# ScalarE in program order through the token-major projections and the indexer of a hybrid decoder step

## The chip, the cores and the metric

The kernel runs on 1 core of one Trainium2 chip. The metric is the device time of one execution in microseconds (us), as the median of several executions. Its instructions sit on five engines with a queue each: TensorE (PE in the profile, with its weight loads as PEld), VectorE (DVE), ScalarE (ACT), GpSimd (POOL) and SyncE (SP). Which engine an instruction belongs to is fixed by the source. The order in which an engine takes its instructions is fixed when the program is built.

## The reference, cut to what matters

One inference step of a 2-layer decoder trunk runs over 1104 tokens of width 1024: 16 meta tokens, 1024 prompt tokens, and 8 sequences of 8 new tokens. Each layer projects the normalised input, runs three mixers, and merges them:

```python
(aq, af, ai, az, b_glu, bz, cq, ck, cv, cqi, cki, cw, cz, gate) = project(h, norm_g, w_in, b_in)
a, g = jnp.split(glu_in, 2, axis=-1)          # conformer_conv, on b_glu
u = a * jax.nn.sigmoid(g)
y = lax.conv_general_dilated(xp, conv_w[:, None, :], ...)      # 31 taps, depthwise, 512 channels
...
qi = rope(cqi.reshape(nb, nt, IDX_HEADS, IDX_DIM), pos)        # 4 heads of 64
ki = rope(cki[:, :, None, :], pos)[:, :, 0]                    # one key head of 64
...
s = jnp.einsum('bqhd,bsd->bqhs', qi, ki)                       # index_scores
scores = jnp.einsum('bqhs,bqh->bqs', jax.nn.relu(s), wi * IDX_SCALE)
idx, valid = select_keys(scores, allowed, n_sel)               # top 256 of the allowed keys
```

The scores pick, for each token, the 256 keys that the sparse attention then reads.

## The kernel before

TensorE works in fp32 through split operands. An operand X is stored as a rounded part and the rest (XH and XL for activations, wh and wl for weights), and a product is three matmuls: wh on XH, wh on XL, wl on XH. ScalarE makes the rounded part by a copy (L269 for the weights of the big projection, L671 for those of the token-major one, L743 for the indexer's keys), GpSimd or ScalarE the rest (L270, L672, L734, L744).

**The stream.** `stream` is a generator that walks over the chunks of the input projection, 128 output channels each. A chunk has three groups of tokens (384, 384 and 336 columns, `g` 0 to 2), a group 24 matmuls (L391), and every third matmul ends in a `yield`. Those three matmuls are called a step here; a group has 8 steps. Behind the 24th matmul ScalarE evicts the group from PSUM into the tile `sp` with bias and activation (L204, called from L394), and behind group 2 ScalarE itself issues the DMA that writes the chunk to DRAM (`fD`). PSUM has two buffers for the groups (`mm`), so a group can't start before the eviction of the group two back has ended.

**Fill.** Everything else of a layer runs in between. `fill(key)` pulls a number of steps from the stream, given by the table `FILL`, so that TensorE has work while another engine prepares what it needs next.

**Taps.** The convolution is VectorE work: 31 taps for each of 4 channel chunks, a tap being two instructions (L1495 on the prompt, L1496 on the samples). `taps(key)` is called between other VectorE work and pulls taps up to a budget in the table `SIDE` ("tr" after each rope of the token-major projections, "tk" and "ti" in the indexer, "ts" in its sample part). At the start of a chunk `gated` loads the two halves of the GLU (`up` and `cy`), ScalarE takes the sigmoid of `cy` in place (`act_(y, y, AF.Sigmoid)`), and GpSimd multiplies. The tile `cy` has two buffers.

**Token-major projections.** `cproj` computes q, k and weights of the indexer and keys and values with tokens on partitions: 2 groups of 290 columns (`gi`) by 9 tiles of tokens (`t`), each 24 matmuls (L679 to L681) into a PSUM buffer from a small ring, a copy by ScalarE into `CTr` (L684), and the bias by GpSimd (L685). For `gi` 1 VectorE then applies the rope (L718 to L722) and pulls taps.

**Indexer.** `indexer` first splits the keys (tile `kk`, named rl in the trace: L733 on ScalarE, L734 on GpSimd), transposes them (L739), and copies them to KIH and KIL (L743, L744, 12 copies). Then come six blocks of 128 queries (`i` from 7 to 2), each with 4 heads. A head is matmuls into the tile `lg` (L770, L771), the next block's transposes when `h == 1` (`qstack`, L757 to L765), `fill("is")` with 6, 4, 7, 6, 7 or 7 steps, and only then the Relu on ScalarE into `rl` (L204), taps, and the weighted sum into `SC` on VectorE (L803 for head 0, L805 for the others). `lg` has one PSUM buffer at this place, so the matmuls of a head wait for the Relu of the head before. `rl` has two buffers. In the source the order is:

```python
fill("is", 7 - i)
rl = xt.tile([128, 1152], F32, name="rl", tag="rl")
act_(rl[:, 0:n], ps[:, 0:n], AF.Relu)
taps("ti", 7 - i)
```

**What sets the order.** TensorE keeps the order in which the source calls its instructions. VectorE does so from the first tap on (`manual_schedule`). For ScalarE, GpSimd and SyncE a scheduler in the compiler chooses the order by its own estimates. Semaphores keep the data right in any order.

Of the kernel before, what the change touches and what calls it, by code (L numbers as in the profile page):

```python
# [11 lines left out]
def _quiet(msg, *args, **kwargs):  # L12
# [10 lines left out]
AF = mybir.ActivationFunctionType  # L23
# [26 lines left out]
SIDE = {"t0": (5000, 10000, 10000, 10000, 9300, 10000), "tr": (4200, 4200, 4200, 4200, 4200, 4200, 4200, 2000, 0),  # L50
# [3 lines left out]
KSEL = 4  # L54
# [100 lines left out]
def trunk(tc, a, o, depth=DEPTH):  # L155
# [47 lines left out]
    def act_(out, in_, fn, **kw):  # L203
        S.activation(out, in_, fn, **kw)  # L204
# [72 lines left out]
    def wpair(l, blk):  # L277
        wh, wl = weights(l, blk)
        return [(lambda k, j=j: wh[:, 2 * k + j, :], lambda k, j=j: wl[:, 2 * k + j, :]) for j in range(2)]
# [61 lines left out]
    def stream(l, pv, chunks, groups, slot, early, lead, more):  # L341


        n = len(chunks)
        blocks = chunks + [("early", (c, bi)) for c in range(8) for bi in range(2)]
        parts = [(c, g) for g in range(3) for c in range(lead)]
        parts += [(i, g) for i in range(lead, n - 2) for g in range(3)]
        parts += [(i, g) for g in range(3) for i in (n - 2, n - 1)]
        parts += [(i, g) for i in range(n, n + 16) for g in range(3)]
        ws, bufs = {}, {}  # L350

        def get(i):
            if i < len(blocks) and i not in ws:
                nm, c = blocks[i]
                if nm == "early":
                    ws[i] = ws[i - 2][1:] if c[0] % 2 else wpair(l, BLK["pb" if c[1] else "pa"] + c[0] // 2)
                else:
                    ws[i] = wchunk(l, BLK[nm] + c, V if i == lead else G, more if 1 < i < lead else None)

        get(0)  # L360
        get(1)
        yield True
        for i, g in parts:
            if g == 0 and 0 < i < lead - 1:
                get(i + 1)
            if lead <= i < n - 1 or i >= n or (i in (lead - 1, n - 1) and g == 2):
                get(i + 1)
            nm, c = blocks[i]
            if nm == "early":
                yield from early.part(c[1], c[0], g, ws[i][0], slot[0])  # L370
                continue
            bcol = BCOL[nm]
            wh, wl = ws[i]
            if g == 0:
                bufs[i] = spt(more if 1 < i < lead else None)
            n0, nn = groups(nm)[g]
            ps = slot[0]()[:, 0:nn]
            sl = slice(n0, n0 + nn)
            H, L = ([x[:, k, sl] for k in range(8)] for x in (XH, XL))
            if i == 0:  # L380

                ops = []
                for k in range(10):
                    if k < 8:
                        ops += [(wh(k), H[k]), (wl(k), H[k])]
                    if k > 1:
                        ops.append((wh(k - 2), L[k - 2]))
            else:
                ops = [(wh(k), x[k]) for k in range(8) for x in (H, L)] + [(wl(k), H[k]) for k in range(8)]
            for j, (w, x) in enumerate(ops):  # L390
                T.matmul(ps, w, x, start=(j == 0), stop=(j == 23))  # L391
                if j == 23:

                    fn = AF.Sigmoid if nm == "gate" and c < 16 else AF.Identity  # L394
                    act_(bufs[i][:, sl], ps, fn, bias=pv[:, bcol + c:bcol + c + 1])
                    if nm in ("cz",):

                        if g == 0:
                            sg = spt()
                        act_(sg[:, sl], ps, AF.Sigmoid, bias=pv[:, bcol + c:bcol + c + 1])  # L400
                        G.tensor_tensor(bufs[i][:, sl], bufs[i][:, sl], sg[:, sl], op=OP.mult)
                    if g == 2:
                        lo = groups(nm)[0][0]
                        S.dma_start(fD[nm][c, :, lo:NT], bufs[i][:, lo:NT])
                    if i == n - 1:
                        early.load(g)
                if j % 3 == 2:
                    yield True

    class Side:  # L410
# [4 lines left out]
        def __call__(self, key, j=0):  # L415
            ns = SIDE[key] if isinstance(key, str) else key
            self.debt += ns[j] if isinstance(ns, tuple) else ns
# [155 lines left out]
    def layer(l, hst, late):  # L573
# [35 lines left out]
        taps = Side(conv(l, pv, cw, cvp))  # L609
# [3 lines left out]
        slot[0] = mmt  # L613
        ctp = ctr.enter_context(tc.tile_pool(name="ctr", bufs=1, side="right"))
        CTr = ctp.tile([128, 9, 580], F32, name="CTr", tag="CTr")
        cproj(l, CTr, taps)
        scp = scs.enter_context(tc.tile_pool(name="scp", bufs=1))
        SC = scp.tile([128, SCN], F32, name="SC", tag="SC")
        SC8 = scp.tile([128, NT], F32, name="SC8", tag="SC8")
        fill("ic")  # L620
        indexer(l, CTr, SC, SC8, fill, taps)
        ctr.close()
        tk1 = tks.enter_context(tc.tile_pool(name="tk1", bufs=1))
        steps, F = topk(SC, SC8, tk1)
# [30 lines left out]
        return merge(l, pv, late_groups, fill, ers)  # L655


    def cproj(l, CTr, taps):
        with tc.tile_pool(name="cpk", bufs=CPK, side="right") as cpk, tc.tile_pool(name="cpr", bufs=2, side="right") as cpr, \
                tc.tile_pool(name="cpt", bufs=2, side="right") as cpt:  # L660
            for gi, (c0, w) in enumerate(CGROUPS):
                brep = cpr.tile([128, 290], F32, name="brep", tag="brep")
                Y.dma_start(brep[:, 0:w], a["b_in"][l, c0:c0 + w].partition_broadcast(128))
                ch, cl = [], []
                for k2 in range(4):
                    cr = cpr.tile([128, 2, 290], F32, name="cr", tag="cr")
                    Y.dma_start(cr[:, :, 0:w], a["wc"][l, gi, k2])
                    for k in range(2):
                        h_ = cpk.tile([128, 290], F32R, name="ch", tag="ch")
                        l_ = cpk.tile([128, 290], F32R, name="cl", tag="cl")  # L670
                        S.copy(h_[:, 0:w], cr[:, k, 0:w])  # L671
                        G.tensor_tensor(l_[:, 0:w], cr[:, k, 0:w], f(h_[:, 0:w]), op=OP.subtract)  # L672
                        ch.append(h_)
                        cl.append(l_)
                for t in range(9):
                    rows, ts = TROWS[t], slice(128 * t, 128 * t + TROWS[t])
                    ps = dmt()
# [786 lines left out]
    def conv(l, pv, cw, c1):  # L1464
        def gated(c):
            up = c1.tile([128, 1070], F32, name="up", tag="up", bufs=2)
            us = c1.tile([128, 8, 38], F32, name="us", tag="us", bufs=2)
            y = c1.tile([128, NT], F32, name="cy", tag="cy", bufs=2)
# [4 lines left out]
            Y.dma_start(y, fD["gg"][c])  # L1473
            Y.dma_start(sr[:, 0], a["state_conv"][l, c])
            G.tensor_copy(us[:, :, 0:30], sr[:, 0])
            act_(y, y, AF.Sigmoid)
            G.tensor_tensor(up[:, 30:1070], up[:, 30:1070], y[:, 0:1040], op=OP.mult)
            G.tensor_tensor(us[:, :, 30:38], us[:, :, 30:38], y[:, 1040:1104].rearrange("p (b q) -> p b q", q=8), op=OP.mult)

# [6 lines left out]
        for c in range(4):  # L1486
            up, us, y = nxt
            yp, ys = y[:, 0:1040], y[:, 1040:1104].rearrange("p (b q) -> p b q", q=8)
            for j in range(31):
                w = cw[:, j, c:c + 1]  # L1490
# [285 lines left out]
```

## Time and profile before

| | |
|---|---|
| time, median of 3 runs | 2926.06 us (2922.28 to 2927.58) |
| the profiled execution's own time | 2926.8 us |
| its span in the profile | 2924.9 us |
| TensorE clock granted, mean | 0.979 of full speed |
| busy share of the span | PE 94%, PEld 90%, DVE 72%, ACT 41%, POOL 43% |

The profile is of one execution. Its own time exceeds its span by 1.9 us of start and end. A busy PE is one with a matmul in its pipeline; the table says that PE seldom stands without one, not how fast it goes. The times below count from the span's start. Layer 0's token-major projections begin at 127.8 us, layer 1's at 1572.5 us.

### The profile page before, as it was taken

How to read it: one execution, taken by the hardware profiler on the slowest of the kernel's cores; microseconds unless marked ns; L12 is line 12 of the kernel's file. 1: busy time of each engine (PE TensorE's matmuls, PEld its weight loads, DVE VectorE, ACT ScalarE, POOL GpSimd, SP SyncE). 2: the span in 40 equal slices, each digit the busy share in tenths (PEclk: the TensorE clock that was granted, in tenths of full speed). 3: DMA queues.
4: the chain of work that ended last, by engine and by line, in shares of the span. 5: the costliest groups of instructions: out<-in, count | busy, mean ns of one | idle time of the engine just before them, and what ended most of it. 6: DMA issues, size and time to landing. Idle time of an engine off the chain costs nothing. (4 is left out here: it accounts for less than half of the span.)

```text
span 2924.9 us, 44993 instructions
## 1 busy us (share of the span) xinstructions
PE 2757.9 (94%) x17094; PEld 2620.9 (90%) x17094; DVE 2113.7 (72%) x3832; ACT 1186.8 (41%) x2369; POOL 1247.6 (43%) x978
## 2 busy tenths in 40 slices
PE   7989899999998999999999998998999999999898
PEld 7988879999998888879999997898999989988798
DVE  5798867889969667535366896788899786774443
ACT  4314443323333556544341334422332335565432
POOL 3533334434425214756564332443434241157563
PEclk9999999999999999999999999999999999999999
DMA  4523234332335124666453322323332441247554
GB/s 146 162 61 109 90 103 140 122 112 89 118 130 170 67 67 154 195 201 197 150 169 105 98 83 90 127 99 109 130 112 77 157 151 63 86 150 222 190 166 148
DMA packets 192569, 374.14 MB, mean 128 GB/s; under 512 B 30657, under 2 KB 129697, under 8 KB 192289
## 3 DMA queue, kind: packets, MB, share of 16 engines
q1 hardware_dynamic: 166016, 272.21, 29.7%
q10 hardware_dynamic: 20448, 78.09, 6.6%
q0 software_dynamic: 5888, 20.97, 2.3%
q8 instruction: 134, 2.20, 0.3%
q14 instruction: 83, 0.67, 0.1%
HBM read 251.07 MB, written 122.40 MB: 128 GB/s over the span
## 5 line engine op out<-in xcount | busy, mean ns | idle before, releaser
L391 PE MATMUL mm<-xh,wh 128*128 128x384 f32 (+2 forms) x2656 | 888.1, 336 | 27.6 <-ACT sp L204 23.9
L391 PE MATMUL mm<-xl,wh 128*128 128x384 f32 (+2 forms) x2656 | 886.0, 336 | 0.0
L270 POOL TENSOR_TENSOR wl<-wr,wh 128x512 fp32r<-128x512 f32 x332 | 473.1, 1443 | 697.8 <-ACT wh L269 465.8
L391 PEld LDWEIGHTS mm<-xh,wh 128*128 128x128 f32 x2656 | 506.0, 191 | 41.5 <-ACT sp L204 29.0
L391 PE MATMUL mm<-xh,wl 128*128 128x384 f32 (+2 forms) x2656 | 531.3, 336 | 0.0
L391 PEld LDWEIGHTS mm<-xl,wh 128*128 128x128 f32 x2656 | 506.2, 191 | 7.2 <-issue 1.9
L391 PEld LDWEIGHTS mm<-xh,wl 128*128 128x128 f32 x2656 | 461.8, 192 | 6.3 <-issue 1.9
L916 DVE TENSOR_SCALAR_CACHE_REDUCE jk<-SC,F 80x1104 bf16<-80x1104 f32 (+6 forms) x448 | 448.8, 1002 | 8.4
L204 ACT ACTIVATE sp<-mm,vec 128x384 f32<-128x384 f32 (+1 forms) x356 | 198.6, 564 | 512.0 <-PE mm L391 494.8
L1495 DVE SCALAR_TENSOR_TENSOR cy<-up,vec,cy 128x1040 f32<-128x1040 f32 x240 | 337.9, 1408 | 0.4
L269 ACT CAST wh<-wr 128x512 fp32r<-128x512 f32 x352 | 203.6, 618 | 164.1 <-PE mm L391 80.4
L204 ACT ACTIVATE P<-P,nm 128x896 f32<-128x896 f32 (+7 forms) x128 | 99.5, 778 | 64.1 <-DVE nm L1021 61.7
L1037 DVE TENSOR_TENSOR pl<-tp,ph 128x512 fp32r<-128x512 f32 x144 | 97.8, 687 | 36.9 <-ACT ph L1036 36.1
L1496 DVE SCALAR_TENSOR_TENSOR cy<-us,vec,cy 128x64 f32<-128x64 f32 x240 | 117.2, 488 | 0.0
L1036 ACT CAST ph<-tp 128x512 fp32r<-128x512 f32 x144 | 83.2, 584 | 54.4 <-PE tp L1033 50.2
L1021 DVE CUSTOM_DVE_ANT_0 P<-sc,MB 128x512 f32<-128x512 f32 (+1 forms) x96 | 63.9, 667 | 57.1 <-PE sc L1015 56.2
L1346 PEld LDWEIGHTS lg<-hQ,hK 128*128 128x128 f32 x512 | 65.8, 205 | 28.0 <-issue 19.9
L1025 DVE TENSOR_SCALAR P<-P,nm 128x896 f32<-128x896 f32 (+7 forms) x128 | 87.4, 683 | 4.3
L1346 PE MATMUL lg<-hQ,hK 128*128 128x64 f32 x512 | 66.4, 286 | 25.5 <-DVE hQ L1375 25.3
L1033 PE MATMUL tp<-ident,P 128*128 128x128 f32 x576 | 88.0, 275 | 1.5 <-DVE P L1025 1.5
L204 ACT ACTIVATE rl<-lg 128x1024 f32<-128x1024 f32 (+6 forms) x54 | 42.6, 788 | 102.8 <-DVE SC L805 60.2
L287 PE MATMUL tp<-xh,wh 128*128 128x384 f32 (+2 forms) x240 | 79.9, 335 | 0.4 <-DVE z L1681 0.4
(454 smaller groups left out, 5932.0 us busy)
## 6 DMA issues: line engine op xcount, KB each, us to landing
wr<-in_wp SPq DMA_DIRECT2D x180, 512.0 KB
eg<-gateD SPq DMA_DIRECT2D x80, 184.0 KB
gateD<-sp ACTq DMA_DIRECT2D x24, 552.0 KB
gateD<-sp ACTq DMA_DIRECT2D x24, 544.0 KB
cr<-in_wc SPq DMA_DIRECT2D x16, 290.0 KB
gt<-gateD SPq DMA_DIRECT2D x24, 192.0 KB
za<-zaD SPq DMA_DIRECT2D x24, 192.0 KB
ggD<-sp ACTq DMA_DIRECT2D x8, 552.0 KB
```

Source lines behind the costliest of these rows:

```text
L204: S.activation(out, in_, fn, **kw)
L269: S.copy(wh[:, k:k + 4], wr[:, k:k + 4])
L270: (eng or G).tensor_tensor(wl[:, k:k + 4], wr[:, k:k + 4], f(wh[:, k:k + 4]), op=OP.subtract)
L391: T.matmul(ps, w, x, start=(j == 0), stop=(j == 23))
L916: V.tensor_scalar(jk[0:rows, 0:n], s, F.bitcast(F32)[0:rows, j:j + 1], None, op0=OP.is_ge, op1=OP.add, accum_out=cnt[0:rows, j:j + 1])
L1025: V.tensor_scalar(p[:, 0:n], p[:, 0:n], nm[:, 3:4], None, op0=OP.mult)
L1033: T.transpose(ps[:, 128 * c:128 * c + 128], P[c][:, 128 * kt:128 * kt + 128], ident)
L1036: S.copy(ph, ps)
L1037: V.tensor_tensor(pl, ps, f(ph), op=OP.subtract)
L1346: T.matmul(ps[:, 64 * c:64 * c + 64], K[:, 128 * c:128 * c + 128], up(Q[:, 128 * c:128 * c + 128], m), start=True, stop=True)
L1495: V.scalar_tensor_tensor(yp, up[:, j:j + 1040], w, yp, op0=OP.mult, op1=OP.add)
L1496: V.scalar_tensor_tensor(ys, us[:, :, j:j + 8], w, ys, op0=OP.mult, op1=OP.add)
```

## The change

Five things are edited. ScalarE's instructions are put under `manual_schedule`, hence in the order of the source, from the first eviction of the token-major projections to the end of the indexer. `cproj` is cut in two loops: the first, outside that order, loads and splits the weights of both groups, the second does the matmuls. For the convolution's chunks 2 and 3 the sigmoid of the GLU's gate half moves from `gated` to the eviction of the projection (`nm == "gg" and c >= 2`), so that DRAM holds the sigmoid already. `SIDE["tr"]` falls by 1000 for each rope, and `SIDE["ts"]` rises by 1000, which moves taps from between the ropes to the indexer's sample part. The lines behind L671 shift by 3 to 8 (in the indexer by 7: L733 is L740 after).

```diff
--- before.py
+++ after.py
@@ -47,8 +47,8 @@
         "hl": (5, 6, 5, 5, 9, 6, 16), "hk": 2, "hs": (0, 1, 0, 1, 0, 1, 0, 4), "ho": 2, "ht": 10, "c0": 59,
         "c1": (13, 22, 52), "aq": 16, "av": (2, 2, 2, 2, 2, 1, 3, 2), "a0": 6, "as": (3, 1, 1, 1, 2, 1, 0, 1),
         "mp": (3, 3, 3), "tl": 3, "tk": 4, "ts": (1, 2, 0, 2, 2), "tt": (0, 0, 1, 4, 6), "tp": (2, 2, 2, 1, 4, 3), "to": 1}
-SIDE = {"t0": (5000, 10000, 10000, 10000, 9300, 10000), "tr": (4200, 4200, 4200, 4200, 4200, 4200, 4200, 2000, 0),
-        "tk": 4200, "ti": (1400, 2800, 2800, 2800, 2800, 2800), "ts": 3000,
+SIDE = {"t0": (5000, 10000, 10000, 10000, 9300, 10000), "tr": (3200, 3200, 3200, 3200, 3200, 3200, 3200, 1000, 0),
+        "tk": 4200, "ti": (1400, 2800, 2800, 2800, 2800, 2800), "ts": 4000,
         "na": (5000, 5000, 5000, 2000, 0, 0, 0, 2000, 1300), "hd": 3000, "hl": (5500, 1000, 2500, 2500, 3700, 4200, 8000),
         "hs": 1000, "hk": 5000, "ho": 500, "ht": 2000, "he": 6500, "c0": 3500, "cc": 1200, "c1": 6000}
 KSEL = 4
@@ -391,7 +391,7 @@
                 T.matmul(ps, w, x, start=(j == 0), stop=(j == 23))
                 if j == 23:
 
-                    fn = AF.Sigmoid if nm == "gate" and c < 16 else AF.Identity
+                    fn = AF.Sigmoid if (nm == "gate" and c < 16) or (nm == "gg" and c >= 2) else AF.Identity
                     act_(bufs[i][:, sl], ps, fn, bias=pv[:, bcol + c:bcol + c + 1])
                     if nm in ("cz",):
 
@@ -613,12 +613,14 @@
         slot[0] = mmt
         ctp = ctr.enter_context(tc.tile_pool(name="ctr", bufs=1, side="right"))
         CTr = ctp.tile([128, 9, 580], F32, name="CTr", tag="CTr")
-        cproj(l, CTr, taps)
+        act = ExitStack()
+        cproj(l, CTr, taps, act)
         scp = scs.enter_context(tc.tile_pool(name="scp", bufs=1))
         SC = scp.tile([128, SCN], F32, name="SC", tag="SC")
         SC8 = scp.tile([128, NT], F32, name="SC8", tag="SC8")
         fill("ic")
         indexer(l, CTr, SC, SC8, fill, taps)
+        act.close()
         ctr.close()
         tk1 = tks.enter_context(tc.tile_pool(name="tk1", bufs=1))
         steps, F = topk(SC, SC8, tk1)
@@ -655,9 +657,10 @@
         return merge(l, pv, late_groups, fill, ers)
 
 
-    def cproj(l, CTr, taps):
+    def cproj(l, CTr, taps, act):
         with tc.tile_pool(name="cpk", bufs=CPK, side="right") as cpk, tc.tile_pool(name="cpr", bufs=2, side="right") as cpr, \
                 tc.tile_pool(name="cpt", bufs=2, side="right") as cpt:
+            groups = []
             for gi, (c0, w) in enumerate(CGROUPS):
                 brep = cpr.tile([128, 290], F32, name="brep", tag="brep")
                 Y.dma_start(brep[:, 0:w], a["b_in"][l, c0:c0 + w].partition_broadcast(128))
@@ -672,6 +675,10 @@
                         G.tensor_tensor(l_[:, 0:w], cr[:, k, 0:w], f(h_[:, 0:w]), op=OP.subtract)
                         ch.append(h_)
                         cl.append(l_)
+                groups.append((gi, c0, w, brep, ch, cl))
+
+            act.enter_context(tc.manual_schedule(engines={mybir.EngineType.Activation}))
+            for gi, c0, w, brep, ch, cl in groups:
                 for t in range(9):
                     rows, ts = TROWS[t], slice(128 * t, 128 * t + TROWS[t])
                     ps = dmt()
@@ -1473,7 +1480,8 @@
             Y.dma_start(y, fD["gg"][c])
             Y.dma_start(sr[:, 0], a["state_conv"][l, c])
             G.tensor_copy(us[:, :, 0:30], sr[:, 0])
-            act_(y, y, AF.Sigmoid)
+            if c < 2:
+                act_(y, y, AF.Sigmoid)
             G.tensor_tensor(up[:, 30:1070], up[:, 30:1070], y[:, 0:1040], op=OP.mult)
             G.tensor_tensor(us[:, :, 30:38], us[:, :, 30:38], y[:, 1040:1104].rearrange("p (b q) -> p b q", q=8), op=OP.mult)
```

TensorE's order is the same in both kernels. VectorE's differs in where taps stand; between the first rope and the last there are 22 before and 16 after. Outside the stretches named above the orders of ScalarE and GpSimd are the same.

ScalarE in layer 0, from the last weight split before the token-major projections to the key split `kk` (`rl<-CTr`). The kernel before:

```order
L684 COPY CTr<-tp 128x290 x2
L204 ACTIVATE cy<-cy 128x1104
L684 COPY CTr<-tp 128x290
L684 COPY CTr<-mm 128x290 x2
L684 COPY CTr<-tp 80x290
L684 COPY CTr<-tp 128x290 x2
L684 COPY CTr<-mm 128x290 x2
L684 COPY CTr<-tp 128x290 x3
L684 COPY CTr<-mm 128x290
L684 COPY CTr<-mm 80x290
L204 ACTIVATE sp<-mm,vec 128x384 x2
L733 CAST rl<-CTr 128x8x64
```

The changed kernel, from the third copy of `gi` 1 on:

```order
L691 COPY CTr<-mm 128x290 x2
L691 COPY CTr<-tp 128x290 x3
L691 COPY CTr<-mm 128x290
L691 COPY CTr<-mm 80x290
L269 CAST wh<-wr 128x512 x2
L204 ACTIVATE sp<-mm,vec 128x384 x2
L204 ACTIVATE sp<-mm,vec 128x336
L404 DMA vD<-sp 128x1104
L269 CAST wh<-wr 128x512 x2
L204 ACTIVATE sp<-mm,vec 128x384
L740 CAST rl<-CTr 128x8x64
L740 CAST rl<-CTr 80x64
```

The sigmoid `cy<-cy`, which stood before between the copies L684, is gone. All three evictions of the first chunk behind the projections, the next chunk's weight split and the first eviction of that chunk now stand ahead of `kk`, where before only two evictions did.

ScalarE in the heads of block `i` 7 (`rl` of 1024 columns; `qs` are the transposed queries). The kernel before:

```order
L404 DMA afD<-sp 128x1104
L204 ACTIVATE rl<-lg 128x1024
L204 ACTIVATE sp<-mm,vec 128x384
L204 ACTIVATE rl<-lg 128x1024
L762 CAST qs<-tp 64x2x128
L763 CAST qs<-tp 64x2x128
L204 ACTIVATE cy<-cy 128x1104
L204 ACTIVATE sp<-mm,vec 128x384
L204 ACTIVATE rl<-lg 128x1024
L269 CAST wh<-wr 128x512 x2
L204 ACTIVATE rl<-lg 128x1024
L204 ACTIVATE sp<-mm,vec 128x336
```

The changed kernel:

```order
L269 CAST wh<-wr 128x512 x2
L204 ACTIVATE sp<-mm,vec 128x384
L204 ACTIVATE rl<-lg 128x1024
L769 CAST qs<-tp 64x2x128
L770 CAST qs<-tp 64x2x128
L204 ACTIVATE sp<-mm,vec 128x384
L204 ACTIVATE rl<-lg 128x1024 x2
L204 ACTIVATE sp<-mm,vec 128x336
L404 DMA aqD<-sp 128x1104
L269 CAST wh<-wr 128x512 x2
L204 ACTIVATE rl<-lg 128x1024
```

Before, the Relu of each of the first heads stands ahead of the eviction `sp` that follows in the stream. After, the eviction stands first: `sp` and then `rl`, twice, and before the fourth Relu the eviction of group 2, its DMA and the next chunk's split.

TensorE at heads 1 and 2 of that block, the same in both kernels (`x8` is eight matmuls in a row; the eighth ends the group):

```order
L391 MATMUL mm<-xh,wh 128x384
L391 MATMUL mm<-xl,wh 128x384
L391 MATMUL mm<-xh,wh 128x384
L391 MATMUL mm<-xl,wh 128x384
L391 MATMUL mm<-xh,wl 128x384 x8
L777 MATMUL lg<-KIH,qs 128x512
L778 MATMUL lg<-KIL,qs 128x512
L777 MATMUL lg<-KIH,qs 128x512
L778 MATMUL lg<-KIL,qs 128x512
```

The group that ends here is the one whose eviction stands ahead of the Relu of head 1, and the matmuls of head 2 (`lg`) follow at once.

VectorE around the last two ropes of the token-major projections (the L718 group is one rope of a tile of tokens). The kernel before:

```order
L718 TENSOR_TENSOR rA<-CTr,cb 128x144
L719 TENSOR_TENSOR rB<-CTr,cb 128x9x8
L720 TENSOR_TENSOR rB<-CTr,cb 128x9x8
L722 TENSOR_TENSOR CTr<-rA,rB 128x2x16
L722 TENSOR_TENSOR CTr<-rA,rB 128x5x16
L1495 SCALAR_TENSOR_TENSOR cy<-up,vec,cy 128x1040
L1496 SCALAR_TENSOR_TENSOR cy<-us,vec,cy 128x64
L1495 SCALAR_TENSOR_TENSOR cy<-up,vec,cy 128x1040
L1496 SCALAR_TENSOR_TENSOR cy<-us,vec,cy 128x64
L718 TENSOR_TENSOR rA<-CTr,cb 80x144
```

The changed kernel:

```order
L1503 SCALAR_TENSOR_TENSOR cy<-up,vec,cy 128x1040
L1504 SCALAR_TENSOR_TENSOR cy<-us,vec,cy 128x64
L725 TENSOR_TENSOR rA<-CTr,cb 128x144
L726 TENSOR_TENSOR rB<-CTr,cb 128x9x8
L727 TENSOR_TENSOR rB<-CTr,cb 128x9x8
L729 TENSOR_TENSOR CTr<-rA,rB 128x2x16
L729 TENSOR_TENSOR CTr<-rA,rB 128x5x16
L725 TENSOR_TENSOR rA<-CTr,cb 80x144
L726 TENSOR_TENSOR rB<-CTr,cb 80x9x8
L727 TENSOR_TENSOR rB<-CTr,cb 80x9x8
```

Between the ropes of `t` 7 and `t` 8 two taps are gone, so the last rope follows the one before at once.

## Rows read from the trace of the kernel before

**Rows 1.** Page: busy time of each engine over the whole span.

```profile
PE 2757.9 (94%) x17094; PEld 2620.9 (90%) x17094; DVE 2113.7 (72%) x3832; ACT 1186.8 (41%) x2369; POOL 1247.6 (43%) x978
```

**Rows 2.** TensorE's waits, layer 0, 110 to 330 us: total, times, longest us.

```profile
PE tp L679 <- ACT CTr L684: 6.2, 1, 6.2
PE mm L391 <- ACT sp L204: 6.0, 2, 4.3
PE lg L770 <- ACT rl L204: 4.1, 4, 1.6
PE tp L777 <- ACT KIL L744: 1.7, 1, 1.7
PE lg L770 <- DVE qs L764: 0.7, 1, 0.7
```

**Rows 3.** Layer 1, 1555 to 1766 us; its row for lg L770 reads alike.

```profile
PE mm L679 <- ACT sp L204: 3.2, 1, 3.2
PE mm L391 <- ACT sp L204: 2.1, 2, 1.7
PE tp L777 <- ACT KIL L744: 2.0, 1, 2.0
PE tp L739 <- POOL rl L734: 1.0, 1, 1.0
```

**Rows 4.** Busy us and instructions by engine, PEclk, DMA: projections, heads, layer 0.

```profile
127.80:194.40 66.60, 60.38 (x434) 60.13 (x433) 62.78 (x91) 8.14 (x20) 24.48 (x24) 0.95 0.18 55
231.60:326.80 95.20, 89.44 (x514) 85.26 (x515) 91.76 (x122) 38.82 (x73) 30.88 (x19) 1.00 0.26 87
```

**Rows 5.** Layer 1: projections, then to the key transposes, then to the first head.

```profile
1572.50:1634.10 61.60, 58.37 (x434) 58.13 (x433) 37.89 (x62) 10.27 (x23) 26.35 (x24) 1.00 0.18 58
1634.10:1652.70 18.60, 18.18 (x107) 17.83 (x106) 18.50 (x36) 3.66 (x7) 8.04 (x6) 1.00 0.27 85
1652.70:1668.10 15.40, 12.32 (x70) 11.71 (x69) 9.18 (x24) 9.13 (x20) 5.35 (x6) 0.89 0.79 239
```

**Rows 6.** Timeline of ACT, layer 0's projections: start, duration, [idle before].

```profile
165.09 1.12 ACT L204 ACTIVATE cy<-cy 128x1104 f32<-128x1104 f32 x1 [20.48 <-DMA cy<-ggD]
```

**Rows 7.** Timeline of PE, layer 0: stall behind the projections, then the key transposes.

```profile
215.18 0.54 PE L391 MATMUL mm<-xh,wh 128*128 128x384 f32 x1 [4.29 <-ACT sp L204]
...
218.07 1.17 PE L739 MATMUL tp<-ident,rl 128*128 128x128 f32 x6
```

**Rows 8.** Timeline of DVE: rope ends, t 0 and 7 (layer 0), 7 (layer 1).

```profile
175.17 0.34 DVE L722 TENSOR_TENSOR CTr<-rA,rB 128x32 f32<-128x32 f32 x2
...
212.60 0.34 DVE L722 TENSOR_TENSOR CTr<-rA,rB 128x32 f32<-128x32 f32 x2
...
1648.43 0.34 DVE L722 TENSOR_TENSOR CTr<-rA,rB 128x32 f32<-128x32 f32 x2
```

**Rows 9.** Groups of ACT, 215 to 350 us: count | busy, mean ns | idle.

```profile
L204 ACT ACTIVATE sp<-mm,vec 128x384 f32<-128x384 f32 x16 | 9.3, 580 | 7.6 <-PE mm L391 7.4
L269 ACT CAST wh<-wr 128x512 fp32r<-128x512 f32 x16 | 9.1, 618 | 5.6 <-PE mm L391 3.1 <-issue 2.4
L204 ACT ACTIVATE rl<-lg 128x1024 f32<-128x1024 f32 x4 | 4.1, 1026 | 4.5 <-PE lg L771 4.4
L204 ACT ACTIVATE rl<-lg 128x384 f32<-128x384 f32 x4 | 1.9, 487 | 6.5 <-DVE SC L805 6.0 <-DVE cy L1495 0.5
```

**Rows 10.** The same for POOL, 205 to 225 us.

```profile
L734 POOL TENSOR_TENSOR rl<-CTr,rl 128x512 f32<-128x512 f32 x1 | 1.6, 1553 | 14.5 <-ACT rl L733 14.5
```

**Rows 11.** Timeline, all engines, around a head's start in layer 1.

```profile
1706.18 0.81 ACT L204 ACTIVATE rl<-lg 128x768 f32<-128x768 f32 x1 [2.83 <-DVE SC L805]
...
1706.89 0.58 ACT L204 ACTIVATE sp<-mm,vec 128x384 f32<-128x384 f32 x1
1707.04 0.19 PEld L770 LDWEIGHTS lg<-KIH,qs 128*128 128x128 f32 x1 [1.12 <-ACT rl L204]
```

## The prediction

> **What bounds the kernel now.** I read the busy shares first: TensorE is busy 94% of the span and VectorE 72% [rows 1], so a stretch gets shorter only where TensorE waits or runs at its lower clock, and longer only where it starts to wait. Then I read TensorE's waits in the stretch that the change touches, once for each layer [rows 2, 3]. The reader is to see that nearly all of them end at ScalarE. Last I read the same stretch by parts, for the granted clock and for VectorE's share [rows 4, 5].
>
> In layer 0 TensorE waits 6.2 us in the token-major projections for a copy L684. ScalarE shows why: it idled 20.48 us at the sigmoid `cy<-cy` for its load, with the copies behind it in its queue [rows 6]. Layer 1 loses 3.2 us at the same place [rows 3]. The same 18 tiles take 66.6 us in layer 0 and 61.6 us in layer 1 [rows 4, 5]. Of the 5.0 us between them the stalls explain 3.0 us; the other 2.0 us is the clock, whose mean in layer 0 is 0.95 of 2.4 GHz against 1.00.
>
> Behind the projections layer 0 waits 4.3 us for an eviction that stands behind the key split, and runs its last nine matmuls before the transposes in 2.9 us, from 215.18 to 218.07 [rows 7], where layer 1's pace of 107 matmuls in 18.6 us [rows 5] gives 1.6 us: 1.2 GHz again. Layer 1 waits 1.0 us for GpSimd's part of the keys and 2.0 us for KIL [rows 3], at a mean clock of 0.89 over 15.4 us [rows 5].
>
> In the heads TensorE waits 4.1 us in each layer for Relus that were late because VectorE was: it is busy 91.76 of 95.20 us there [rows 4], and the Relu of rows 11 had waited 2.83 us for `SC`. Some 2 us in each layer are other waits (0.7 and 1.7 in layer 0, 2.1 in layer 1) [rows 2, 3].
>
> **The projections.** With the sigmoid gone and ScalarE in the source's order, each copy runs as soon as its matmuls end. The two stalls go: 6.2 + 2.0 us in layer 0, 3.2 us in layer 1. The sigmoid in the eviction replaces an Identity there, one instruction for one, and costs nothing; the eviction has a whole group of cover. If it had none, six evictions of 0.58 us [rows 9] a layer would bound it. The weight split that moves behind the projections (two copies of 0.62 us [rows 9]) is needed three groups later, some 12 us, which covers it and GpSimd's part behind it.
>
> **The key split.** It now stands behind all evictions of one chunk and the first of the next. In layer 1 TensorE reaches the transposes 3.2 us earlier, at 1652.7 - 3.2 = 1649.5. The rope it needs ended at 1648.8 [rows 8] and will end earlier. The eviction ahead of the split ends about 0.9 us before that (nine matmuls, 1.6 us, less some 0.7 for the eviction), then 0.62 us of ScalarE (as a `wh` of this size [rows 9]) and 1.55 us of GpSimd [rows 10]: 1650.8. A new stall of 1.3 us, and a gain of 1.9 us at this point. The second GpSimd part then waits for no late rope: 1.0 us. KIL follows at once, with some 0.5 us left of the 2.0: 1.5 us. The half clock goes: 0.11 of 15.4 us is 3.4 us at half, so up to 1.7 us; I take 1.6. Layer 1: 6.0 us.
>
> In layer 0 the ropes decide. From the end of the first at 175.5 to the end of the eighth at 212.9 are 37.4 us with 20 taps and seven ropes [rows 8]: a tap is under 1.87 us, and about 1.55 with the ropes taken out. Four taps fewer make 6.2 us, the missing sigmoid of 1.12 us lets the first rope start about as much earlier, so the eighth ends at 205.5. With 2.2 us of split the transposes start at 207.7, against 218.07: 10.4 us. TensorE would be there at 194.4 - 8.2 + 18.6 = 204.8, so a stall of 2.9 us is left. KIL 1.2 us and the rest of the half clock 0.3 us come on top: 11.9 us. Were a tap 1.4 us and the sigmoid worth nothing, it would be 10.2; if TensorE met no stall at all, 14.8.
>
> A page of the Trainium skill bears on the clock here ("TensorE: Matmul & The Clock Gate", section "Part 1: The HAM clock gate"): low is the default, work releases it, idleness brings it back, and the monitor's windows run free of the kernel. By that rule a stall of 2.9 us may still draw the low clock or not, and the sum would be 1.5 us higher where it does. The rows show both: low behind 4.3 us, not low in layer 1's projections with a stall of 3.2 us.
>
> **The heads.** This is the cost. In the source a head's `lg` matmuls are followed by fill steps and only then by the Relu, so in program order an eviction that falls into these steps stands ahead of the Relu. `lg` has one buffer: TensorE's next head waits for the Relu, which waits for the eviction, which waits for matmuls that TensorE does after this head. Before, the scheduler put the Relu first. With r whole steps left between the evicted group and the next head, the wait is 0.2 (start of the eviction, an estimate; it lies between 0 and 0.4) + 0.48 (0.58 less the 0.10 by which instructions overlap, 1706.89 against 1706.99 [rows 11]) + the Relu (1.03 us for 1024 columns, 0.49 for 384 [rows 9], in proportion between) + 0.05 (end of Relu to TensorE, 1706.99 to 1707.04 [rows 11]) - 0.52 r (three matmuls at the pace of rows 5). At a chunk's end the DMA issue (0.3 us, an estimate) and mostly two weight copies, 1.15 us, stand there too.
>
> TensorE's order gives r for each of the 24 heads. Ten have no eviction or enough steps behind it. The others, in us: block 7, 0.7 (r = 2), 1.8 (r = 0, the place shown above) and 1.0 (chunk's end, r = 4); block 6, 1.65 twice (r = 0); block 5, 1.3 (chunk's end, r = 3), 0.5, 1.0 and 1.85 (r = 0, DMA issue); block 4, 0.4 and 1.75; block 3, 0.6; block 2, 0.2 and 2.1. That is 16.5 us a layer. With the start of the eviction at 0 or 0.4 it is 14 to 19. VectorE's lateness doesn't add to it: its 91.8 us and one tap more fit into heads that last some 105 us, so its 4.1 us vanish. The 1.7 us before an eviction behind the sample copies go as well, and of the first wait for `qs` 0.5 us stay. Before 6.5 and 6.2 us, after 17.0 each: a loss of 21.3 us.
>
> Taps moved into the sample part number about five a layer; VectorE waits for TensorE there, and I cost them at nothing. Without that cover it would be five times 1.5 us a layer.
>
> **The sum.** 2926.8 - 11.9 - 6.0 + 21.3 = 2930.2 us on the profiled execution's own time, which lies 0.7 above the median. I predict 2930. A measurement can tell 0.2%, 5.9 us, from no change.
>
> **Rivals.**
>
> *The heads don't pay.* The evictions are done so soon that the Relu is late by little, and waits stay near 6 us a layer. For it: before, ScalarE always kept up; it is busy 38.82 of 95.20 us [rows 4]. Against it: the eviction can't start before its group ends, and at r = 0 the next head follows directly. The time would be 2926.8 - 17.9 = 2909. It decides for "faster" once the heads cost less than 12.5 us a layer.
>
> *The clock falls in the heads.* Six stalls of 1.65 us and more a layer now stand where it was 1.00 [rows 4]. A fall costs 1.5 to 2.0 us as worked out above. Two a layer give 2936, six give 2950; one in all takes it past 0.2%. Against it: stalls of 1.6 us in the heads drew none before [rows 2, 4]. The same page, section "HAM oscillation", describes a loop in which every wait between bursts brings the low clock back; by that it would be the 2950. The trace so far bears it out only for longer stalls.
>
> *The projections still stall.* The copies meet another late instruction. Then 11.4 us of gain are missing: 2941. Nothing in ScalarE's new order shows one.
>
> **How the numbers follow.** The sum as it stands, with its bounds, 0.50 (2923 to 2938: 2.5 us a layer for the heads' formula, 2 us for the key split); heads that don't pay 0.22; falling clock 0.20; projections 0.08. The range from 2911 to 2942 leaves out half of the first rival and a third of the second. Faster by over 0.2% is nearly all of the first rival and little else: 0.25. Within it lies over half of the likeliest case and the edges of others: 0.35. Slower: 0.40.
>
> **What would show it.** TensorE waiting neither for L691 nor an eviction in the projections; waits of 1 to 3 us for L741's output at the transposes; in the heads some 14 waits for `rl`, with `sp` directly ahead of it on ScalarE, and VectorE idle there for 10 us. The prediction is wrong if those waits sum to under 12 or over 20 us, if the clock row of the heads falls below 1.00, or if something late in the layers moves.

## The result, and the profile after

The changed kernel takes 2941.73 us (median of 6 runs, 2936.10 to 2947.01) against 2925.42 us before (6 runs, 2922.28 to 2927.58): a ratio of 1.0057, with a 95% interval of 1.0043 to 1.0072. It is slower by 16 us. The prediction was 2930 us, no change that a measurement can tell, and gave "slower" 0.40. The time lies at the very end of its range.

The profiled execution took 2947.0 us and has a span of 2945.2 us, 20.3 more than before. TensorE's waits in the stretch of the change, layer 0 to 330 us and then layer 1 from 1545 to 1790 us (total, times, longest, in us), answer to [rows 2, 3]:

```profile
PE lg L777 <- ACT rl L204: 13.2, 12, 1.8
PE tp L746 <- POOL rl L741: 9.0, 1, 9.0
...
PE lg L777 <- ACT rl L204: 15.3, 13, 2.1
PE tp L746 <- POOL rl L741: 1.0, 1, 1.0
PE tp L784 <- ACT KIL L751: 0.4, 1, 0.4
```

The waits of the projections are gone in both layers. In the heads there are 13 waits for `rl` where there were four (layer 0's thirteenth, of 2.1 us, ends at 334.4 us, behind the stretch of its row). In layer 0 one wait of 9.0 us has appeared at the key transposes.

By stretch (columns as in [rows 4]): the projections, the way to the first head (two rows, parted at the key transposes) and the heads of layer 0, then the heads of layer 1, and the sample part of both layers. The last two rows are the sample part of the kernel before.

```profile
127.88:186.00 58.12, 58.12 (x433) 58.12 (x433) 53.90 (x75) 7.39 (x18) 23.02 (x24) 1.00 0.19 55
186.00:213.08 27.08, 18.04 (x108) 17.73 (x106) 26.77 (x52) 5.49 (x10) 10.37 (x8) 0.92 0.23 77
213.08:226.14 13.06, 13.06 (x69) 12.93 (x69) 6.46 (x18) 8.53 (x19) 0.51 (x2) 0.78 0.72 218
226.14:334.41 108.27, 92.83 (x515) 86.17 (x514) 94.58 (x123) 37.23 (x66) 29.43 (x23) 0.98 0.25 86
...
1672.12:1780.49 108.37, 92.94 (x515) 86.33 (x514) 94.63 (x129) 37.08 (x66) 29.31 (x23) 0.98 0.25 86
...
334.50:384.00 49.50, 41.39 (x213) 35.68 (x214) 27.33 (x37) 22.04 (x37) 16.44 (x13) 0.90 0.24 77
1780.50:1828.00 47.50, 39.41 (x212) 33.70 (x213) 27.21 (x37) 21.83 (x37) 16.41 (x13) 0.93 0.26 81
...
326.80:371.00 44.20, 38.09 (x213) 32.37 (x212) 28.38 (x39) 21.48 (x31) 16.75 (x13) 0.96 0.34 110
1763.10:1807.50 44.40, 37.81 (x212) 32.11 (x212) 28.21 (x39) 21.29 (x31) 16.77 (x13) 0.96 0.35 109
```

With the same borders before, the profile's 20 us come apart as follows (us, after minus before, and what the prediction's terms gave for it; the "way to the first head" is from the projections' end to the first `lg`, and the sample part from the last head's first matmul to the last transposes of gathered keys, which lie up to 0.8 us inside the rows' rounded borders):

| stretch | layer 0 | forecast | layer 1 | forecast |
|---|---|---|---|---|
| projections | -8.5 | -8.2 | -3.5 | -3.2 |
| way to the first head | +2.9 | -3.7 | -3.9 | -2.8 |
| heads | +13.1 | +10.5 | +13.4 | +10.8 |
| sample part | +5.2 | 0 | +2.9 | 0 |

The projections came as forecast, and layer 1's way 1.1 us better. The three others did not: they are 19.9 us above their terms, and with what went better elsewhere the profile is 16.8 us off.

**Layer 0's way to the first head.** The timeline of VectorE and then of GpSimd in the changed kernel, at the rope of `t` 3, at the second pair of subtractions (200.03) and at the end of the eighth rope (start, duration):

```profile
187.09 4.15 DVE L729 TENSOR_TENSOR CTr<-rA,rB 128x32 f32<-128x32 f32 x2
191.17 1.30 DVE L1503 SCALAR_TENSOR_TENSOR cy<-up,vec,cy 128x1040 f32<-128x1040 f32 x1
...
202.44 2.35 DVE L1503 SCALAR_TENSOR_TENSOR cy<-up,vec,cy 128x1040 f32<-128x1040 f32 x1
...
210.63 0.34 DVE L729 TENSOR_TENSOR CTr<-rA,rB 128x32 f32<-128x32 f32 x2
...
187.84 0.71 POOL L692 TENSOR_TENSOR CTr<-CTr,brep 80x290 f32<-80x290 f32 x1
188.50 2.54 POOL L270 TENSOR_TENSOR wl<-wr,wh 128x512 fp32r<-128x512 f32 x2
...
200.03 3.66 POOL L270 TENSOR_TENSOR wl<-wr,wh 128x512 fp32r<-128x512 f32 x2 [7.86 <-ACT wh L269]
```

Two small additions of a rope, 0.34 us elsewhere [rows 8], take 4.15 us. They end just behind GpSimd's subtractions (191.24 and 191.04). These two subtractions belong to the chunk whose split the change moved from ahead of the projections to behind them. The next chunk's pair stands among the ropes as well, where it stood behind the eighth rope before; beside it the two instructions at 201.20 and 202.44 take 1.32 and 2.35 us instead of 0.28 and 1.30. The eighth rope ends at 211.0 us in this layer, not at the forecast 205.5, and TensorE waits 9.0 us where 2.9 were forecast. The clock then falls: 0.78 of full speed over the 13.06 us behind that wait.

**A head.** All engines in the changed kernel at the end of head 1 of block 7 (the place shown in the section on the change):

```profile
235.51 0.58 ACT L204 ACTIVATE sp<-mm,vec 128x384 f32<-128x384 f32 x1 [2.41 <-PE mm L391]
235.99 1.02 ACT L204 ACTIVATE rl<-lg 128x1024 f32<-128x1024 f32 x1
237.04 1.28 DVE L812 SCALAR_TENSOR_TENSOR SC<-rl,wsc,SC 128x1024 f32<-128x1024 f32 x1 [1.52 <-ACT rl L204]
237.06 0.50 PE L777 MATMUL lg<-KIH,qs 128*128 128x512 f32 x1 [1.59 <-ACT rl L204]
```

ScalarE stood idle for 2.41 us before the eviction with the Relu behind it, runs both, and TensorE goes on 0.05 us after the Relu. It is the chain of the prediction's formula.

### The profile page after: what moved, and what is told of

The parts are those of the page before. It is cut to its first block, busy times and chain, and to the rows that moved or that the text cites. A ratio compares the mean times of both kernels' runs of the same rounds, so it can differ in the third digit from the quotient of the medians.

```text
span 2945.2 us, 44981 instructions
## 1 busy us (share of the span) xinstructions
PE 2763.1 (94%) x17094; PEld 2620.9 (89%) x17094; DVE 2114.9 (72%) x3832; ACT 1183.9 (40%) x2365; POOL 1245.6 (42%) x978
## 5 line engine op out<-in xcount | busy, mean ns | idle before, releaser
L1504 DVE SCALAR_TENSOR_TENSOR cy<-us,vec,cy 128x64 f32<-128x64 f32 x240 | 103.2, 430 | 0.0
L1353 PE MATMUL lg<-hQ,hK 128*128 128x64 f32 x512 | 67.7, 290 | 21.7 <-DVE hQ L1382 21.5
L287 PE MATMUL tp<-xl,wh 128*128 128x384 f32 (+2 forms) x240 | 78.1, 328 | 0.0
```

What stands on the lines that cost most here:

```text
L287: T.matmul(ps[:, 0:nn], wk, x, start=(n == 0), stop=(n == 3 * K - 1))
L1353: T.matmul(ps[:, 64 * c:64 * c + 64], K[:, 128 * c:128 * c + 128], up(Q[:, 128 * c:128 * c + 128], m), start=True, stop=True)
L1504: V.scalar_tensor_tensor(ys, us[:, :, j:j + 8], w, ys, op0=OP.mult, op1=OP.add)
```

## The experiments

All times are medians. Ratios are against the kernel before on the same chip. That base is 2924.23 us for the first four runs (up to "No fixed order"), 2926.87 us for the next four (up to the old taps) and 2924.01 us for the last three, so times of different groups are best compared by their ratios.

**The Relu ahead of the fill steps.** In `indexer`:

```diff
-                    fill("is", 7 - i)
                     rl = xt.tile([128, 1152], F32, name="rl", tag="rl")
                     act_(rl[:, 0:n], ps[:, 0:n], AF.Relu)
+                    fill("is", 7 - i)
```

> The changed kernel with one edit: in the heads the Relu is called ahead of the fill steps, so in ScalarE's program order it stands ahead of the evictions that fall into them. TensorE's and VectorE's orders stay. Theory 1 (program order put the evictions ahead of the Relu, and this costs the heads 10 us a layer, with 2 to 3 us more by the clock): the waits of lg for rl fall from 13.2 and 15.3 us to about 4 as before, the heads from 108.3 to about 95 us a layer, and the kernel runs at about 2918 us (2913 to 2923). Theory 2 (the heads are longer for another reason, as VectorE or contention): the heads keep 105 us or more and the time stays above 2935.

Measured: 2908.11 us, ratio 0.9952 (0.9935 to 0.9969). Its waits in layer 0 to 320 us, and its heads there:

```profile
PE tp L746 <- POOL rl L741: 7.0, 1, 7.0
PE lg L777 <- ACT rl L204: 3.1, 4, 1.3
...
221.83:314.05 92.22, 89.10 (x515) 85.08 (x515) 89.20 (x115) 36.31 (x64) 31.38 (x22) 1.00 0.26 90
```

One moved line turns a kernel slower by 16 us into one faster by 16 us. The heads take 92.2 us: less than the 108.3 of the change, and less than the 95.2 before [rows 4]. Theory 1 holds for the cause. The time is below its 2913 to 2923 us, as the waits in layer 0's heads are 3.1 us and not the 6.5 us of before, and the wait for L741 is 7.0 us and not 9.0 (why that one is shorter was not tried). The heads of both layers together are 32.2 us shorter, which is most of the gain (33.6 us by the medians, 39.6 by the two profiles).

**The early split.** The chunk's weights are fetched and split before the fixed order begins (`stream.get` is the generator's own `get`):

```diff
+            stream.get(9)
             act.enter_context(tc.manual_schedule(engines={mybir.EngineType.Activation}))
```

> The changed kernel with one edit: the weight split of the chunk that begins three groups behind the projections is called before ScalarE's order is fixed, so it stands ahead of the projections as in the kernel before. Theory 1 (GpSimd's two subtractions wl of that split, running among the ropes at 188.5 to 191 us, held VectorE's rope for 4.0 us in layer 0): the rope L729 near 187 us takes 0.2 us instead of 4.0, the wait for L741 in layer 0 falls from 9.0 us to about 5.3, layer 1 is unchanged at 1.0, and the kernel gains 3 to 4 us: about 2938. Theory 2 (the ropes are late by themselves): the wait stays at 8 to 9 us and the time at 2942.

> Both edits, the Relu ahead of the fill steps and the early weight split. If the two costs are separate they add: about 2914 us (2909 to 2920), with heads of 95 us a layer and a wait of about 5 us for L741 in layer 0. If one hides the other, the time is no better than that of the Relu's edit alone.

Measured: 2944.08 us, ratio 1.0063 (1.0042 to 1.0083), and with the Relu's edit 2906.03 us, 0.9932 (0.9915 to 0.9949). Neither differs beyond the spread from the kernel that it edits, so the time is that of theory 2. In the first of the two, the rope of `t` 3, the start of the first rope, and the wait in layer 0:

```profile
189.97 0.34 DVE L731 TENSOR_TENSOR CTr<-rA,rB 128x32 f32<-128x32 f32 x2
...
174.23 2.10 DVE L727 TENSOR_TENSOR rA<-CTr,cb 128x144 f32<-128x144 f32 x1 [4.12 <-POOL CTr L694]
...
PE tp L748 <- POOL rl L743: 7.9, 1, 7.9
```

The long rope is gone, as theory 1 said, but the first rope starts at 174.23 where it started at 171.85 in the changed kernel, and the wait falls by 1.1 us instead of 3.7. Put ahead of the projections, the pair of subtractions (128.36 to 131.90 us) holds VectorE's taps there by some 2 us. On this chain a pair costs VectorE some 2 to 4 us at each place it had, so moving it gains little. With the Relu's edit the wait does not fall at all: 7.8 us against 7.0. My expected size was wrong.

**No fixed order.** The line with `manual_schedule` for ScalarE is taken out, and the rest of the change stays.

> The changed kernel without ScalarE's fixed order; the sigmoid in the eviction, the two loops and the moved taps stay. The scheduler then puts the key split L739 right behind the last projection copy, ahead of two evictions. Theory 1 (the sigmoid alone caused the stalls in the projections; the fixed order alone causes the cost of the heads): no stall in the projections, heads of about 95 us, but a stall of some 10 us in layer 0 and 4 us in layer 1 for the evictions that stand behind L739, which waits for the ropes; about 2919 us. Theory 2 (the fixed order is needed for the projections too): stalls of 3 to 6 us there remain and the time is near 2926.

Measured: 2922.40 us, ratio 0.9991 (0.9981 to 1.0001). TensorE's waits in layer 0, and ScalarE's wait ahead of the key split:

```profile
PE mm L391 <- ACT sp L204: 15.0, 2, 13.8
PE lg L776 <- ACT rl L204: 4.6, 5, 2.3
...
206.92 0.62 ACT L739 CAST rl<-CTr 128x512 fp32r<-128x512 f32 x1 [20.57 <-DVE CTr L728]
```

No wait is left in the projections, and the heads take 96.7 us (clock 0.98). One wait of 13.8 us has come: the scheduler puts the key split, which waits for the ropes, ahead of two evictions. So the cost of the heads comes with the fixed order, and the order's worth is that it keeps those evictions free.

**The changed kernel once more.**

> The changed kernel itself once more, one profile. Its times so far range from 2936 to 2947 us. If falls of the clock at stalls near the edge make that spread, TensorE's waits are the same to 0.2 us each, the heads last 106.7 us a layer where the clock shows 1.00 and about 1.5 us more for a fall in them, and the time follows the number of falls. If something else makes it, waits differ.

Measured: 2945.38 us in one run. The waits are the same (13 for `rl`, 15.3 us), but for L741 (9.3 us, 0.3 more). Its heads, of layers 0 and 1, are shorter:

```profile
223.34:330.06 106.72, 91.31 (x514) 84.73 (x513) 94.93 (x129) 37.16 (x66) 29.18 (x23) 1.00 0.26 87
1667.21:1774.04 106.83, 91.40 (x514) 84.81 (x513) 94.81 (x129) 37.07 (x66) 28.89 (x23) 1.00 0.26 87
```

With equal waits, the heads are 1.5 us shorter where the clock did not fall (0.98 against 1.00). This part of the expectation holds. That the time follows these falls does not: this run is only 1.6 us shorter in all, and the clock differs elsewhere as well (0.99 against 0.96 over the first 120 us, 0.97 against 0.99 from 400 to 600 us).

**The sigmoid back.** On the kernel with the Relu's edit, the eviction is Identity again and `gated` takes all four sigmoids:

```diff
-                    fn = AF.Sigmoid if (nm == "gate" and c < 16) or (nm == "gg" and c >= 2) else AF.Identity
+                    fn = AF.Sigmoid if nm == "gate" and c < 16 else AF.Identity
...
-            if c < 2:
-                act_(y, y, AF.Sigmoid)
+            act_(y, y, AF.Sigmoid)
```

> The kernel with the Relu ahead of the fill steps, and the sigmoid taken back out of the eviction into the convolution's preparation, as before the change; ScalarE's order stays fixed. Theory 1 (the sigmoid that waits for its load, with the copies behind it, made the stalls in the projections): in program order it stands among the copies again, TensorE waits there for 3 to 10 us a layer, and the kernel loses 8 to 20 us: about 2920 us. Theory 2 (a fixed order suffices): no such stall, time within 3 us of 2908.

Measured: 2909.21 us, ratio 0.9935 (0.9910 to 0.9960). Theory 1 falls. ScalarE's timeline in layer 0:

```profile
170.39 0.40 ACT L691 COPY CTr<-mm 128x290 f32<-128x290 f32 x1 [2.83 <-PE mm L688]
170.69 1.13 ACT L204 ACTIVATE cy<-cy 128x1104 f32<-128x1104 f32 x1
```

In the source's order the sigmoid stands eight copies later than the scheduler had put it (13 copies L691 ahead of it instead of five). Its load has landed by then, and it runs without a wait in a gap of ScalarE. The stall is gone with the sigmoid moved and no fixed order, and with the fixed order and the sigmoid in its old place. Both kernels keep the two loops and the moved taps; whether these alone would do was not tried.

**The sample part.** On the kernel with the Relu's edit, `act.close()` moves into `indexer`, behind the six blocks:

```diff
+            act.close()
             _, lo8, hi8 = nxt
```

> The kernel with the Relu ahead of the fill steps, with ScalarE's fixed order ended behind the six blocks of heads, so that the scheduler orders the indexer's sample part. Theory 1 (the fixed order also costs the sample part, by the weight split ahead of the copies kib and by the sample copies all behind the last heads): the wait at the third gather for kib falls from 1.5 to 0.6 us, but the eviction ahead of the last head is again delayed by the sample copies by up to 1.7 us; in sum 1 to 2 us a layer better or equal, 2904 to 2909. Theory 2 (the sample part was longer only by the clock and the gathers): no change beyond 1 us.

Measured: 2913.68 us, ratio 0.9950 (0.9931 to 0.9969), not faster than 2908.11. The waits of its sample part in layer 0, and of its base:

```profile
PE tp L896 <- DMA kir<-in_cache_kidx,rowid: 4.2, 2, 3.9
PE tp L896 <- ACT kib L901: 2.3, 2, 1.7
PE mm L391 <- ACT sp L204: 1.6, 1, 1.6
```

```profile
PE tp L895 <- DVE cy L1503: 4.0, 1, 4.0
PE tp L895 <- ACT kib L900: 3.2, 2, 1.7
PE tp L895 <- DMA kir<-in_cache_kidx,rowid: 1.2, 1, 1.2
```

The wait for `kib` falls by 0.9 us and a wait of 1.6 us for an eviction takes its place, both as theory 1 said; the waits ahead of the gathered keys fall from 5.2 to 4.2 us in this layer and stay in the other (4.6 and 4.7). They cancel: in each layer the sample part up to its first matmul on `qt` is 2.1 us shorter (67.7 and 67.1 us against 69.8 and 69.2), and the heads are 2.0 us longer (94.2 against 92.2). By the ratios (0.9950 and 0.9952) the time is the same.

**The taps.** On the kernel with the Relu's edit, once with the table before the change, once with another step in the change's direction (cut to the values; in the order of the lines added):

```diff
-        "tr": (3200, 3200, 3200, 3200, 3200, 3200, 3200, 1000, 0), "ts": 4000
+        "tr": (4200, 4200, 4200, 4200, 4200, 4200, 4200, 2000, 0), "ts": 3000
+        "tr": (2200, 2200, 2200, 2200, 2200, 2200, 2200, 0, 0), "ts": 5000
```

> The kernel with the Relu ahead of the fill steps, with the table of taps as before the change, so that six more taps stand between the ropes. Theory 1 (in layer 0 the ropes on VectorE decide when the key split starts, in layer 1 they don't): the wait for L741 in layer 0 rises from 7.0 by 6 to 9 us and in layer 1 from 1.0 by 0 to 5 us; the time is 2914 to 2920 us. Theory 2 (taps between the ropes are covered): within 3 us of 2908.

> The kernel with the Relu ahead of the fill steps, and the table of taps changed once more by the change's own amount: another 1000 less for each rope, another 1000 more in the sample part. Theory 1 (layer 0's ropes decide, and taps in the sample part are covered by VectorE's waits for TensorE): the wait for L741 in layer 0 falls from 7.0 to about 1 us; about 2902 us. Theory 2 (the sample part has no cover left): the wait falls as well, but the first gather, or the topk behind, waits for VectorE by 5 to 10 us a layer, and the time is 2908 or more.

Measured: 2913.32 us, 0.9956 (0.9942 to 0.9970), with the old taps; 2901.17 us, 0.9916 (0.9895 to 0.9938), with fewer. The wait of layer 0's transposes, first with the old taps and then with fewer:

```profile
PE tp L746 <- POOL rl L741: 13.8, 1, 13.8
```

```profile
PE tp L746 <- POOL rl L741: 1.4, 1, 1.4
```

From 13.8 over 7.0 to 1.4: six taps fewer between the ropes and then five (22, 16 and 11), worth 6.8 and 5.6 us of this wait. The sample part pays nothing back: TensorE's first wait there, for VectorE or the gather, is 4.1 us with fewer taps and was 4.0 with the Relu's edit alone. The taps decide this wait, and their new place is covered. In the time only the second step shows, and that narrowly: the ratio goes from 0.9956 over 0.9952 to 0.9916.

**VectorE subtracts.** With both edits of the early split, the rest of the weights of the two chunks behind the projections is made by VectorE itself (`V if i in (lead, 9, 10) else G`); then this together with the fewer taps.

> The kernel with both edits (Relu ahead of the fill steps, early split), and VectorE instead of GpSimd subtracts the rest wl for the two chunks behind the projections, once ahead of the first rope's taps and once behind the last rope. Theory 1 (GpSimd's pairs of wl hold VectorE's instructions for 2 to 4 us each, and so made layer 0's ropes late): the eighth rope in layer 0 ends 3 to 4 us earlier, the wait for L741 falls from 7.8 to about 4 us, and the time from 2906 to about 2902. Theory 2 (they don't matter, the taps alone do): the wait stays at 7 to 8 us, or rises by the 1 to 2 us of VectorE's own subtractions.

> Relu ahead of the fill steps, early split, VectorE's subtractions and the fewer taps together. If taps and subtractions are both on the path to the key split, the wait for L741 in layer 0 falls to that of layer 1, about 1 us, and not below, so this is no better than the better one of the two by more than 2 us: 2899 to 2903 us. If the taps in the sample part are not covered, 2905 to 2912 us.

Measured: 2909.28 us, 0.9943 (0.9922 to 0.9965), and 2900.43 us, 0.9914 (0.9890 to 0.9937). The wait of layer 0's transposes in the first of the two, then the end of its eighth rope, and the end of that rope with both edits alone:

```profile
PE tp L748 <- POOL rl L743: 4.3, 1, 4.3
...
205.69 0.34 DVE L731 TENSOR_TENSOR CTr<-rA,rB 128x32 f32<-128x32 f32 x2
...
209.88 0.34 DVE L731 TENSOR_TENSOR CTr<-rA,rB 128x32 f32<-128x32 f32 x2
```

It falls from the 7.8 us of both edits to 4.3 us. The eighth rope ends at 206.0 us instead of 210.2, of which 0.8 us is an earlier start of the projections: GpSimd's subtractions did hold VectorE. The median shows nothing of the 3.5 us; the runs reach from 2901.50 to 2915.51. With the fewer taps, nothing is left to gain there (1.0 us of wait), and the time is that of the fewer taps alone. At 2901 us both are faster than the kernel before by some 23 us and than the changed one by 40.

## Why the prediction was wrong

**The failed step: the split behind the projections.** The prediction said that it "is needed three groups later, some 12 us, which covers it and GpSimd's part behind it". That covers TensorE, which indeed doesn't wait for these weights. It named no cover for VectorE. GpSimd's pair ran among the ropes and held one of them for 3.8 us, and the next pair cost 2.1 more. Together that is 5.9 us, about what the eighth rope was late (5.5). Since layer 0's ropes decide when the key split can start, the stall was 9.0 us instead of 2.9. It was made of taps and subtractions, as the old taps, the fewer taps and VectorE's own subtractions showed (13.8, 1.4 and 4.3 us of wait). The range I gave for this term moved only the price of a tap, the sigmoid's worth and where TensorE would be. Two of these were a little too high as well: away from GpSimd's work a tap takes 1.41 us and not 1.55, and the first rope ended 0.5 us earlier and not 1.1.

The Trainium skill has the rule that I passed over ("SBUF — State Buffer", section "Who interferes with whom"): a VectorE instruction with two inputs in SBUF and a GpSimd instruction that reads SBUF exclude each other, and the later one waits. The trace agrees that the two exclude each other, but not on which waits: one rope addition, 4.00 us of the 4.15, starts at 187.09, ahead of three GpSimd instructions in a row, 187.84 to 191.04, and ends behind them all (until 187.81 GpSimd issues a gather). GpSimd's times in a profile are rough, so which of the two was issued first stays open.

**The heads: right in mechanism, a little small.** The formula gave 16.5 us of waits a layer and the profile has 15.3, counted from the matmuls' modelled ends. At full clock the heads lasted 106.7 and 106.8 us against 95.2 and 95.0 before, so 11.5 and 11.8 us and not 10.5 and 10.8. That VectorE's lateness would vanish is right. That the order of Relu and evictions is the cause is shown by the one moved line.

**The clock.** The rival of a falling clock came in part. In the profiled run the heads lost 1.5 us a layer by it, to one fall in each (in layer 0 the mean clock is 0.72 of full speed from 282 to 286 us, 0.85 from 286 to 290, and 1.00 around them), and layer 0 stood at 0.78 behind the 9.0 us wait. So the clock row of the heads, 0.98, met the prediction's own sign of being wrong, while the sum of the waits, 15.3 us, did not. A second profile of the same kernel with the same waits shows none in the heads. I had it at 0.20, with two falls a layer as its mild case; a fall at every wait, its 2950, is not what these rows show.

**The sample part: a second failed step, put at nothing.** With 8.1 us in both layers it is the largest miss of the profile. I asked whether taps are covered there, which they are, and not what ScalarE's order does to it. It puts a chunk's weight split ahead of the copies `kib`: those waits rise from 2.3 to 3.2 us a layer, the gathers' from 3.9 and 4.3 to 4.9. That is 1.9 and 1.5 us. The waits in layer 0's sample part, before and after:

```profile
PE tp L888 <- DMA kir<-in_cache_kidx,rowid: 3.9, 2, 3.6
PE tp L888 <- ACT kib L893: 2.3, 2, 1.7
...
PE tp L895 <- DMA kir<-in_cache_kidx,rowid: 4.9, 2, 4.5
PE tp L895 <- ACT kib L900: 3.2, 2, 1.7
```

The rest of the 5.2 and 2.9 us goes with the clock, 0.96 before and 0.90 and 0.93 after: by my estimate from these rows, a mean that is 0.10 and 0.07 short of full speed costs up to 5.0 and 3.3 us, and 1.8 us before. Why the clock is lower there and why the gathers come 0.6 to 1.0 us later was not tried, so this part of the cause stays open.

**The projections: right.** Both stalls and the half clock went (8.5 and 3.5 us). I laid this to the sigmoid's absence and the source's order together; the runs without one of the two show that either is enough.

**The other rivals.** "The heads don't pay" and "the projections still stall" are refuted by the rows above.

**The sum.** 3.4 us were forecast on the profiled execution and 20.2 measured. The 16.8 us between them are 6.6 from the ropes and what follows them in layer 0, 5.2 from the heads (3.1 of it clock) and 8.1 from the sample part, less 1.7 for what went better and 1.4 between layer 0's sample part and layer 1's projections. Over the six runs of each kernel the change is 16.3 us.

## What to carry to other kernels

When an engine is put into program order, look at each tile with one buffer: its release must be called ahead of any work that waits for another engine's later instructions. Here one line's place was worth some 33 us. When a step moves, ask of every engine that it runs on who runs beside it there, not only who waits for its result: cover for TensorE was none for VectorE. And see which chain ends last at the place before pricing an instruction on it, since a tap was worth 1.1 us of TensorE's wait among the ropes and nothing in the sample part.

## What was not expected of the hardware

VectorE's two additions of a rope, 0.34 us elsewhere, lasted 4.15 us beside a bias addition and two subtractions of 512 columns on GpSimd, and a tap's first instruction beside such a pair took 2.35 us (202.44 us in the changed kernel) instead of 1.30. So here instructions of two engines that share neither data nor a semaphore (the subtractions and the ropes) were on one critical path.

Two profiles of one kernel with equal waits in the heads differ in where the clock stands at 1.2 GHz: 0.98 and 1.00 of full speed over the same 107 to 108 us, which is 1.5 us.
